# Adding the last block of the seven-product down step into x: from VectorE to a ScalarE copy and accumulating DMAs

## The chip, the core and the metric

The kernel runs on one core of a Trainium2 chip. The metric is the time of one launch in microseconds of the device. The core has TensorE (PE: matrix products into PSUM; its weight loads, PEld, run beside them), VectorE (DVE), ScalarE (ACT), GpSimd (POOL) and SyncE (SP). They run side by side, each its own list of instructions in order, and wait for one another by semaphores. Sixteen DMA engines move data; here SP issues the loads of the weights, and POOL issues the DMAs that add what they carry to what lies at their destination (accumulating DMAs).

## The reference, cut to what matters

The reference is one inference step of an encoder with two layers, for 512 new frames of one stream and 16 frames of each of eight running streams: 640 columns in all. Each layer is a half-step feed-forward block, a mixer (a short convolution and a banded attention with gates), and a second half-step feed-forward block:

```python
def _swiglu(h, w_gu, w_down):
    gu = h @ w_gu
    g, u = jnp.split(gu, 2, axis=-1)
    return (jax.nn.silu(g) * u) @ w_down
...
xp = xp + 0.5 * _swiglu(_rmsnorm(xp, norm_ffn1[l]), w_ffn1_gu[l], w_ffn1_down[l])
```

D_MODEL is 1024, D_FF is 2816, everything is float32. The change lies in the last product of this function, `@ w_down`, and in how its result, times a half, gets into x.

## The kernel before, in words

**Layout.** x lies in SBUF as eight tiles of 128 rows (of the 1024 features) by 640 columns (the frames). The columns are halved: `t1` is the first 320, `t2` the second. A float32 product is made of three faster ones: each operand is split into a high and a low part (`hi`, `lo`), and high x high, high x low and low x high are summed in PSUM.

**Weights.** One long stream of weights, laid out ahead, is loaded by SP (`load`, L236) into tiles `raw` of 512 KB, of which three exist. ACT copies the high part (`whi`, L296), DVE subtracts it from the tile to get the low part (`wlo`, L301); three tiles of each exist. When its `wlo` is done, a `raw` tile is free for the next load. SP's loads are in the order of the stream, and each waits for its buffer.

**Seven products for eight.** In most of the feed-forward blocks' steps a 2 x 2 block product is made with seven block products instead of eight (a Strassen-like scheme). Its blocks are named X11, X21, XN6, XT5, XT7, X22, XT4, and they are run in this order, each as 12 matmuls; each needs its own combination of weights and of activations. The combinations of weights are summed by DVE (`add`, L240; in the profile `s<-raw`, `s<-s,raw`, `raw<-raw,raw`, `raw<-s,raw`). A block's result goes into several outputs, so PSUM banks are read in the middle of their accumulation, and the next block on the same bank waits until that is done.

**Gate/up.** `gate_up` runs the seven blocks for one group of 128 features of the hidden layer: X11, XN6, XT7 and XT4 accumulate on one after the other in the bank `pa`, X21 in `pb`, XT5 and X22 in `pc`. ACT copies `pa` after X11 into c1 (L819). After XT7 DVE adds `pa` and the copy c5 into g (`add(g[:, t2], pa, c5)`, in the profile `ga<-paa,c_a` or `gb<-pab,c_b`), and XT4, the last block, goes on in `pa`. Between XT7 and XT4 there is one block, X22.

**Down.** `down_rows` does the same for four tiles of x at a time: its banks are A (`a`, two halves of 320 columns; `daa` and `dab` in the profile, for the two layers), B (`b`) and `c`. The results go into x in two ways. `take` is DVE: x = scale * bank + x, two instructions of 128 x 320 (L980). `stage` is ACT: a copy of the bank, with the factor, into a tile of SBUF with the tag `cap` (L967 for both halves of A in one instruction, L970 for the two c banks); then `send` issues two accumulating DMAs of 160 KB on POOL (L975), which add the two halves of the copy to two tiles of x. Before the change, of seven reads of the banks three are staged (c1 after X11, u2 after XN6, c5 after XT5) and four are takes (b after X21, a after XT7, c after X22, a after XT4). Three sends, that is six DMAs, belong to a call.

**Order.** The hidden features come in chunks, of four groups in the seven-product part. In a chunk the gate/up steps of this chunk and the down products of the chunk before are run in turn: gate/up, gate/up, down for x tiles 0 to 3 ("first call"), gate/up, down for x tiles 4 to 7 ("second call"), gate/up. There are 26 calls of `down_rows`, 13 first and 13 second, in four feed-forward blocks (6, 6, 8 and 6). In this part the order of PE's instructions is fixed by hand (`order({PE})`, a manual schedule of PE alone); where DVE's and ACT's instructions stand is decided by the Tile framework's scheduler, which places them by its own estimate of when each can run. `prep`, `flush`, `ahead` and `slab` are the functions that issue the weights' loads and splits a few blocks ahead.

Of the kernel before, what the change touches and what calls it, by code (L numbers as in the profile page):

```python
# [165 lines left out]
def two(ps):  # L166
    return ps[:, :, :HT]
# [7 lines left out]
def trunk(ctx: ExitStack, tc: tile.TileContext, xin, wst, small, pbias, samplebias, kcache, vcache,  # L175
# [24 lines left out]
    def acc(name):  # L200
        return banks["acc"].tile([P, 2, 512], F32, tag="acc", name=name)

    def att(name):
        return banks["att"].tile([P, 512], F32, tag="att", name=name)
# [78 lines left out]
    def prep(i):  # L283

        if i < len(ready) or i >= len(slabs):
            return
        assert i == len(ready)
        parts = source(i)
        hi = wp.tile([P, CH], F32R, tag="whi", name=f"whi{i}", bufs=3)
        lo = wp.tile([P, CH], F32R, tag="wlo", name=f"wlo{i}", bufs=3)  # L290
        ready.append((hi, lo))
        o = 0
        for src, c in parts:
            d = slice(o, o + c.stop - c.start)
            o = d.stop
            ACT.copy(hi[:, d], src[:, c])  # L296
            pending.append((lo[:, d], src[:, c], hi[:, d]))

    def flush():
        for lo, src, hi in pending:  # L300
            DVE.tensor_tensor(out=lo, in0=src, in1=hi.bitcast(F32), op=ALU.subtract)  # L301
        pending.clear()
# [3 lines left out]
    def slab(hold=False):  # L306

        flush()
        i = used[0]
        used[0] += 1  # L310
        while len(ready) < min(i + 2, len(slabs)):
            prep(len(ready))
            flush()
        prep(i + 2)
        if not hold:
            flush()
        return ready[i], slabs[i]

    def ahead():

        source(len(ready))

    def begin():

        prep(used[0] + 2)

    def quiet():

        used[0] += 1
        return ready[used[0] - 1]  # L330
# [599 lines left out]
    def step(later, place):  # L930

        for p in later:
            while p.done < 5 and p.spots[p.done] == place:
                next(p.work)
                p.done += 1

    def down_rows(fp, n, ms, pairs, tails, later):


        A, B = (acc(f"d{i}{n}") for i in "ab")  # L940
        a, b = ([z[:, u, :HT] for u in range(2)] for z in (A, B))
        c = [att(f"dc{n}_{u}")[:, :HT] for u in range(2)]
        t1, t2 = slice(0, HT), slice(HT, T)
        second = ms[0] > 0

        def mul(ps, s, half, kind, start):
            for u in range(2):
                for i, pair in enumerate(pairs):
                    kp = half * NP + 2 * u + i
                    wh, wl = (z[:, kp * P : (kp + 1) * P] for z in s)  # L950
                    xh, xl = pair.X[kind]
                    for j, (w, y) in enumerate(((wh, xh), (wh, xl), (wl, xh))):
                        PE.matmul(ps[u], w, y, start=start and i == 0 and j == 0,  # L953
                                  stop=i == 1 and j == 2, skip_group_check=True)

        def place(name):
            step(later, f"r{int(second)}{name}")

        def tail():
            for t in tails:  # L960
                t(False)
            tails.clear()

        def stage(name, ps, scale=0.5):
            z = fp.tile([P, 2, HT], F32, tag="cap", name=f"{name}{n}", bufs=5)
            if ps is A:
                ACT.activation(z, two(A), AF.Copy, scale=scale)  # L967
            else:
                for u in range(2):
                    ACT.activation(z[:, u], ps[u], AF.Copy, scale=scale)  # L970
            return z

        def send(z, r, cols):
            for u in range(2):
                POOL.dma_start(x[ms[2 * u + r]][:, cols], z[:, u], accum_op=ALU.add)  # L975

        def take(ps, r, cols, scale=0.5):
            for u in range(2):
                xs = x[ms[2 * u + r]][:, cols]
                DVE.scalar_tensor_tensor(out=xs, in0=ps[u], scalar=scale, in1=xs, op0=ALU.mult, op1=ALU.add)  # L980

        s0 = quiet()
        mul(a, s0, 0, X11, True)
        c1 = stage("c1_", A)
        prep(used[0] + 1)
        begin()
        if not second:
            tail()
        flush()
        place("d1")  # L990
        mul(b, s0, 1, X21, True)
        take(b, 0, t1)
        send(c1, 0, t1)
        s1 = slab(True)[0]
        flush()
        mul(a, s1, 0, XN6, False)
        u2 = stage("u2_", A)
        mul(c, s1, 1, XT5, True)
        c5 = stage("c5_", c, -0.5)
        s2 = slab(True)[0]  # L1000
        if second:
            tail()
        mul(a, s2, 0, XT7, False)
        take(a, 1, t2, -0.5)
        send(c5, 1, t2)
        flush()
        ahead()
        mul(c, s2, 1, X22, False)
        take(c, 0, t2)
        send(u2, 0, t2)  # L1010
        s3 = slab(True)[0]
        ahead()
        mul(a, s3, 0, XT4, False)
        take(a, 1, t1, -0.5)
        flush()

    def ffn(name, fp, ex, goff, after, end=False):
# [19 lines left out]
        for what, a in ffn_order(name):  # L1037
# [19 lines left out]
            if what == "rows":  # L1057
                ms, js = a
                down_rows(fp, f"{name}_{js[0]}_{ms[0]}", ms, [pairs[j] for j in js[::2]], tails, later)
                continue  # L1060
# [825 lines left out]
```

## Time and profile before

| | |
|---|---|
| median of 3 runs | 2536.31 us (2536.09 to 2536.59) |
| profiled execution | 2537.11 us, span 2535.3 us |
| TensorE's granted clock | 0.999 |
| busy: PE / DVE / ACT / POOL | 2512.6 / 2116.1 / 1271.9 / 198.1 us |
| DMA queue of POOL's software DMAs (q0) | 35.36 MB, 7.8% of 16 engines over the span |
| DMA queue of SP's loads (q1) | 223.90 MB, 27.3% |

The span is the time from the first to the last instruction of the profiled execution; what the whole execution took is 1.8 us more. A row of the groups reads: line, engine, operation, output <- inputs, count, duration in ns as min/median/max, first and last start in us, shape. A row of the waits reads: who waited, at which output and line, for whom; then the sum in us, how often, and the longest. A row of the timeline reads: start in us, duration in us, engine, line, operation, count; at its end, in brackets, how long the engine was idle before it and what ended that. A row of the DMA view with "KB" gives the line's transfers, their size, and the time from issue to landing. In the code after the change every line below L937 has a number higher by one.

### The profile page before, as it was taken

The page shows a single profiled execution, that of the slowest core. Times are in us where ns is not written, and L with a number is a line of the kernel's source. Part 1 is how long each engine was busy: PE and PEld are TensorE (multiplying, and loading weights), DVE is VectorE, ACT ScalarE, POOL GpSimd, SP SyncE. Part 2 cuts the span into 40 slices and gives each one's busy share as a digit, 9 for nine tenths or more (in the row PEclk, how much of TensorE's full clock was granted, in tenths as well). Part 3 has the DMA queues.
Part 4 walks back from the last instruction along what each step waited for, and adds up shares of the span by engine and source line. Part 5 has one row for each costly group of instructions (what it writes and reads, how often), then busy time and mean ns, then how long its engine had stood idle before and what let it go on. Part 6 is the DMA issues. An engine that isn't in the chain of part 4 may idle for free. (4 is left out here: it accounts for less than half of the span.)

```text
span 2535.3 us, 43090 instructions
## 1 busy us (share of the span) xinstructions
PE 2512.6 (99%) x17264; PEld 2451.2 (97%) x17264; DVE 2116.1 (83%) x3389; ACT 1271.9 (50%) x2010; POOL 198.1 (8%) x309
## 2 busy tenths in 40 slices
PE   8999999999999999999999999999999999999998
PEld 8999999888999999999999999998889999999998
DVE  7789998778777998998789999987786778999975
ACT  5345555664444545544455555556644445455543
POOL 0001111111000001110000111101110000011100
PEclk9999999999999999999999999999999999999999
DMA  3234343235222134443222444333442222244432
GB/s 135 67 100 115 108 121 112 106 112 171 76 76 92 64 112 113 107 110 99 84 84 92 120 118 115 105 105 118 134 137 84 76 85 78 97 115 115 116 99 75
DMA packets 96536, 262.65 MB, mean 104 GB/s; under 512 B 10736, under 2 KB 41584, under 8 KB 96336
## 3 DMA queue, kind: packets, MB, share of 16 engines
q1 hardware_dynamic: 70272, 223.90, 27.3%
q0 software_dynamic: 25344, 35.36, 7.8%
q8 instruction: 135, 2.21, 0.4%
q10 hardware_dynamic: 720, 0.65, 0.1%
q14 instruction: 65, 0.53, 0.1%
HBM read 225.85 MB, written 7.94 MB: 92 GB/s over the span
## 5 line engine op out<-in xcount | busy, mean ns | idle before, releaser
L296 ACT CAST whi<-raw 128x1024 fp32r<-128x1024 f32 (+1 forms) x566 | 506.1, 898 | 387.8 <-PE pcb L386 50.0
L301 DVE TENSOR_TENSOR wlo<-raw,whi 128x1024 fp32r<-128x1024 f32 (+1 forms) x566 | 581.7, 1031 | 120.8 <-ACT whi L296 115.2
L296 ACT CAST whi<-s 128x1024 fp32r<-128x1024 f32 (+1 forms) x146 | 138.0, 945 | 266.7 <-DVE s L240 113.8
L386 PE MATMUL pab<-xhib,whi 128*128 128x320 f32 x704 | 218.3, 310 | 1.3 <-DVE gb L240 1.0
L386 PE MATMUL pab<-xhib,wlo 128*128 128x320 f32 x704 | 217.2, 309 | 0.0
L386 PE MATMUL pab<-xlob,whi 128*128 128x320 f32 x704 | 217.2, 309 | 0.0
L386 PE MATMUL paa<-xhia,whi 128*128 128x320 f32 x640 | 198.0, 309 | 0.8 <-ACT c_a L766 0.6
L386 PE MATMUL paa<-xloa,whi 128*128 128x320 f32 x640 | 197.4, 308 | 0.0
L386 PE MATMUL paa<-xhia,wlo 128*128 128x320 f32 x640 | 197.4, 308 | 0.0
L301 DVE TENSOR_TENSOR wlo<-s,whi 128x1024 fp32r<-128x1024 f32 (+1 forms) x146 | 158.7, 1087 | 13.1 <-ACT whi L296 13.1
L386 PEld LDWEIGHTS pab<-xhib,whi 128*128 128x128 f32 x704 | 132.1, 188 | 2.5 <-DVE gb L240 1.2
L386 PEld LDWEIGHTS pab<-xlob,whi 128*128 128x128 f32 x704 | 132.1, 188 | 0.2
L386 PEld LDWEIGHTS pab<-xhib,wlo 128*128 128x128 f32 x704 | 132.1, 188 | 0.0
L240 DVE TENSOR_TENSOR s<-raw 128x512 f32<-128x512 f32 x110 | 75.7, 688 | 63.9 <-DMA raw<-in_wst 63.5
L386 PEld LDWEIGHTS paa<-xhia,whi 128*128 128x128 f32 x640 | 120.0, 187 | 1.6 <-ACT c_a L766 0.8
L975 POOL DMA_DIRECT2D x<-c_b x48 | 41.9, 956 | 1002.8 <-ACT whi L296 921.7
L386 PEld LDWEIGHTS paa<-xloa,whi 128*128 128x128 f32 x640 | 120.0, 188 | 0.1
L386 PEld LDWEIGHTS paa<-xhia,wlo 128*128 128x128 f32 x640 | 120.0, 187 | 0.0
L975 POOL DMA_DIRECT2D x<-c_a x56 | 49.1, 957 | 814.8 <-ACT whi L296 740.3
L386 PE MATMUL pcb<-xhib,whi 128*128 128x320 f32 x352 | 108.6, 309 | 0.0
L386 PE MATMUL pcb<-xlob,whi 128*128 128x320 f32 x352 | 108.6, 309 | 0.0
L386 PE MATMUL pcb<-xhib,wlo 128*128 128x320 f32 x352 | 108.6, 309 | 0.0
(686 smaller groups left out, 7894.7 us busy)
## 6 DMA issues: line engine op xcount, KB each, us to landing
raw<-in_wst SPq DMA_DIRECT2D x384, 512.0 KB, 3.5
x<-c_a POOLq DMA_DIRECT2D x56, 160.0 KB, 3.4
kc<-in_kcache SPq DMA_DIRECT2D x32, 256.0 KB, 4.0
vc<-in_vcache SPq DMA_DIRECT2D x16, 512.0 KB, 4.9
x<-c_b POOLq DMA_DIRECT2D x48, 160.0 KB, 3.4
x<-u_a POOLq DMA_DIRECT2D x28, 160.0 KB, 4.3
bias<-in_pbias POOLq DMA_DIRECT2D x16, 256.0 KB, 3.7
x<-u_b POOLq DMA_DIRECT2D x24, 160.0 KB, 4.4
```

The lines of the kernel that those rows point to most:

```text
L240: DVE.tensor_tensor(out=out, in0=a, in1=b, op=ALU.add)
L296: ACT.copy(hi[:, d], src[:, c])
L301: DVE.tensor_tensor(out=lo, in0=src, in1=hi.bitcast(F32), op=ALU.subtract)
L386: PE.matmul(ps, a, b, start=start and kp == 0 and j == 0, stop=stop and kp == NP - 1 and j == 2, skip_group_check=True)
L975: POOL.dma_start(x[ms[2 * u + r]][:, cols], z[:, u], accum_op=ALU.add)
```

## The change

The last read of bank A in `down_rows`, behind the block XT4, was a take by DVE: two instructions of 128 x 320 which add -0.5 times the bank to the first halves of two tiles of x. Now ACT copies the bank, times -0.5, into a new tile `c4_` with the tag `cap` in one instruction of 128 x 640, and POOL issues two accumulating DMAs of 160 KB. It is the same sum; x's tiles get it by another engine. Per call that is two DVE instructions fewer, one ACT instruction more and two POOL DMAs more.

```diff
@@ -937,6 +937,7 @@
     def down_rows(fp, n, ms, pairs, tails, later):
 
 
+
         A, B = (acc(f"d{i}{n}") for i in "ab")
@@ -1011,7 +1012,7 @@
         s3 = slab(True)[0]
         ahead()
         mul(a, s3, 0, XT4, False)
-        take(a, 1, t1, -0.5)
+        send(stage("c4_", A, -0.5), 1, t1)
         flush()
```

## The prediction

> **What bounds the kernel now.** I read the busy times first, then what PE waits for, then the timeline of the stretch around the changed step.
>
> ```profile
> span 2535.3 us, 43090 instructions
> PE 2512.6 (99%) x17264; PEld 2451.2 (97%) x17264; DVE 2116.1 (83%) x3389; ACT 1271.9 (50%) x2010; POOL 198.1 (8%) x309
> ```
>
> PE is busy for 2512.6 of 2535.3 us, and the change leaves its instructions and their order alone. So it can move the time only by what PE waits for. The rows of the waits that belong to the down products and the gate/up step behind them (times: sum in us, count, longest):
>
> ```profile
> PE daa L953 <- DVE x L980: 1.4, 7, 0.2
> PE dab L953 <- DVE x L980: 1.2, 6, 0.2
> PEld daa L953 <- DVE x L980: 3.2, 7, 0.5
> PEld dab L953 <- DVE x L980: 2.7, 6, 0.5
> PE pab L386 <- DVE gb L240: 1.0, 1, 1.0
> DVE s L240 <- DMA raw<-in_wst: 63.5, 37, 3.1
> ```
>
> PE stands at two kinds of place. The 13 stops of the first two rows are seen again at its weight loader, whose records overlap PE's, with 5.9 us, so that one costs about 0.46 us. The last row is DVE's own wait: 37 times it stands for a weight tile, 63.5 us in all. That is no loss yet, but PE waits for what stands behind it.
>
> The removed instructions, and the kind that takes their place on ACT:
>
> ```profile
> L980 DVE SCALAR_TENSOR_TENSOR x<-daa,x x56: 479/482/493, 221.2 to 1649.3; 128x320 f32<-128x320 f32 x56
> L980 DVE SCALAR_TENSOR_TENSOR x<-dab,x x48: 477/481/492, 977.8 to 2404.5; 128x320 f32<-128x320 f32 x48
> L967 ACT ACTIVATE c_b<-dab x12: 683/687/710, 970.7 to 2393.2; 128x640 f32<-128x640 f32 x12
> ```
>
> Half of the 104 go: two in each of 26 calls. Now one gate/up step behind such a call (the second call of its chunk). It starts at 323.53; its XT7 block starts at 330.57 and its XT4 block at 334.09, 3.52 us later:
>
> ```profile
> 323.73 0.89 DVE L980 SCALAR_TENSOR_TENSOR x<-daa,x 128x320 f32<-128x320 f32 x2
> ...
> 326.80 1.22 DVE L301 TENSOR_TENSOR wlo<-raw,whi 128x1024 fp32r<-128x1024 f32 x1
> 328.05 1.33 SPq L236 DMA_DIRECT2D raw<-in_wst  x2
> 330.57 0.31 PE L386 MATMUL paa<-xhia,whi 128*128 128x320 f32 x1
> 331.41 0.69 DVE L240 TENSOR_TENSOR s<-raw 128x512 f32<-128x512 f32 x1 [2.39 <-DMA raw<-in_wst]
> ...
> 333.15 0.48 DVE L240 TENSOR_TENSOR ga<-paa,c_a 128x320 f32<-128x320 f32 x1
> 333.55 0.68 DVE L240 TENSOR_TENSOR s<-s,raw 128x512 f32<-128x512 f32 x1
> 334.09 0.31 PE L386 MATMUL paa<-xhia,whi 128*128 128x320 f32 x1
> ```
>
> The reader is to see a chain. The end of `wlo<-raw` (328.02) frees a buffer, so SP issues the load (328.05); `s<-raw` waits for it until 331.41; behind it in DVE's queue stand a `wlo` and `ga<-paa`, and XT4 overwrites the bank that `ga<-paa` reads. That read ends at 333.63, so only 0.46 us are left.
>
> **The change part by part.** In the compiled order of the changed kernel PE and SP have the same instructions in the same order; DVE has 52 fewer, ACT 26 more, POOL 52 more.
>
> (1) The two takes. The pair holds DVE for up to 0.89 us from 323.73 on. DVE was behind here, so the two `wlo` and the buffer's release come up to that much earlier. Bounds: 0 (the next `wlo` waits for ACT instead) to 0.89. I take 0.7, since DVE had no idle time recorded between these rows.
>
> (2) The copy. 26 x 0.69 us on an ACT that is half idle. It waits for the same last product as the takes did. Behind it on ACT stand the `whi` of later weights and gate/up's c1 copy:
>
> ```profile
> 2404.07 1.05 ACT L296 CAST whi<-raw 128x1024 fp32r<-128x1024 f32 x1 [1.26 <-PE dab L953]
> 2405.84 0.43 ACT L819 COPY c_b<-pab 128x320 f32<-128x320 f32 x1 [0.72 <-PE pab L386]
> ```
>
> ACT was idle for 1.26 and 0.72 us there, so 0.69 us is taken up before c1. I take 0; were that cover gone, c1 could cost PE up to 0.69 x 26 = 18 us at XN6, which overwrites what c1 reads.
>
> (3) The two sends. POOL has only the sends to issue here:
>
> ```profile
> 2402.16 1.76 POOL L975 DMA_DIRECT2D x<-c_b  x2 [4.15 <-DVE x L980]
> 2403.30 2.40 POOL L975 DMA_DIRECT2D x<-u_b  x2
> ```
>
> The c4 pair stands behind the pair `x<-u_b`, and I put its issue at about 2.4 us more, which nobody waits for: the tile of x is next read much later, and ACT's tiles come around some 14 us apart (estimate from five buffers and about five copies to a call). What counts is the 16 DMA engines, where the pair meets the load of the chain above. Windows of the DMA view (20 quiet us; 10 us around four sends, two of u and two of c; two loads beside sends, packets of the queue or issue to landing in us):
>
> ```profile
> q1 hardware_dynamic: 431, 1.57, 25.8%
> raw<-in_wst SPq DMA_DIRECT2D x4, 512.0 KB, 3.4
> ```
> ```profile
> q0 software_dynamic: 583, 0.66, 44.4%
> ```
> ```profile
> raw<-in_wst SPq DMA_DIRECT2D x1, 512.0 KB, 4.2
> ```
> ```profile
> raw<-in_wst SPq DMA_DIRECT2D x1, 512.0 KB, 5.0
> x<-c_b POOLq DMA_DIRECT2D x2, 160.0 KB, 6.0
> ```
>
> A send is 128 packets; 583 took 44.4% of 10 us, so a pair (256) takes 4.44 x 256 / 583 = 1.95 us of all engines. A load alone lands in 3.4 us; beside sends in 4.2 (the gate/up from 2378.78, behind the tail of u2's pair) and 5.0 (two sends beside it). So a load that meets a whole pair is between 0 (if loads go first) and 1.95 us longer; I take 1.5, near the 5.0 row, because the c4 pair follows u2's directly and covers the load's whole time.
>
> [...]
>
> (4) DVE's order. Tile places DVE's instructions anew, and in the changed order the second sum `s<-s,raw` stands ahead of `wlo` and `g<-pa` in all 24 steps behind a call that have such a sum; before, in 6. One of those six shows the longer chain:
>
> ```profile
> 2385.82 0.31 PE L386 MATMUL pab<-xhib,whi 128*128 128x320 f32 x1
> 2386.04 0.69 DVE L240 TENSOR_TENSOR s<-raw 128x512 f32<-128x512 f32 x1 [2.30 <-DMA raw<-in_wst]
> 2386.77 0.69 DVE L240 TENSOR_TENSOR s<-s,raw 128x512 f32<-128x512 f32 x1
> 2387.38 1.22 DVE L301 TENSOR_TENSOR wlo<-raw,whi 128x1024 fp32r<-128x1024 f32 x1
> 2388.51 0.48 DVE L240 TENSOR_TENSOR gb<-pab,c_b 128x320 f32<-128x320 f32 x1
> ```
>
> From the start of `s<-raw` to the end of `gb<-pab` it is 2.95 us. PE therefore waits as soon as `s<-raw` starts later than 3.52 - 2.95 = 0.57 us behind XT7.
>
> (5) The 0.46 us stops ahead of the down products' own XT4 stay. They come from `take(a, 1, t2)`, which is not touched, and in the second calls the order ahead of it is the same:
>
> ```profile
> 2399.94 1.23 DVE L301 TENSOR_TENSOR wlo<-raw,whi 128x1024 fp32r<-128x1024 f32 x1 [0.46 <-ACT whi L296]
> 2401.09 0.88 DVE L980 SCALAR_TENSOR_TENSOR x<-dab,x 128x320 f32<-128x320 f32 x2
> 2402.02 0.41 PE L953 MATMUL dab<-t4hib,whi 128*128 128x320 f32 x1 [0.20 <-DVE x L980]
> ```
>
> In five first calls a sum moves ahead of this take and uses up the room; 0 to 0.5 us each, I take 0.
>
> The sum. Second calls: in 9 of the 11 with a sum `s<-raw` starts like the first, 331.41 - 330.57 = 0.84 us behind XT7, and up to 0.93. There the load met no send. The queue of the sends was as good as empty from 327.5 to 329.5:
>
> ```profile
> q0 software_dynamic: 6, 0.01, 2.0%
> ```
>
> So the load is longer by the whole 1.5 and starts 0.7 earlier: net +0.8, or +0.3 if a third of the pair is past by then. I take +0.6: the wait is 0.87 + 0.6 - 0.57 = 0.9 us, 9 x 0.9 = 8.1. The other two start earlier:
>
> ```profile
> 2410.58 0.69 DVE L240 TENSOR_TENSOR s<-raw 128x512 f32<-128x512 f32 x1 [1.73 <-DMA raw<-in_wst]
> ```
>
> XT7 there is at 2410.92; from -0.3 the load's 1.5 with little gain brings about +0.9, some 0.3 each, 0.6. First calls: 13 starts, the first and the last 0.17 and 0.22 behind XT7 (231.07 and 2385.82), all between -0.75 and 1.04, the middle one 0.48.
>
> ```profile
> 231.24 0.69 DVE L240 TENSOR_TENSOR s<-raw 128x512 f32<-128x512 f32 x1 [2.25 <-DMA raw<-in_wst]
> ```
>
> The load met u2's tail already (4.2), so only 5.0 - 4.2 = 0.8 is new and 0.7 is won: net +0.1 to +0.2. Only the four latest (0.57 to 1.04, mean 0.77) pass 0.57 clearly, by 0.35: 1.4, less what is only reached. Sum 8.1 + 0.6 + 1.4 = 10.1 us, and I take 9.5, since the sends may come in part behind the load. The profiled execution took 2537.11 us (span 2535.3 and 1.8 around it), 0.8 above the median of the runs; 2537.1 + 9.5 = 2546.6 answers to 2545.8 as a median. One in 500 (5.1 us) is about what a measurement can tell from no change.
>
> **The rivals.** (A) The load is hardly held, and the earlier release pays for it: a shift of -0.4 to 0. Then the moved sum alone costs 9 x (0.87 - 0.2 - 0.57) = 0.9 to 2.7 us and the first calls next to nothing: +2, 2538.3, no change. For it speaks that SP's load is issued up to 0.9 us earlier, at a time when u2's pair may be the only one in the engines; against it the 5.0 row. (B) The other side. The stops of (5) vanish because DVE, 0.9 us less laden, reaches `take(a, 1, t2)` in time: 13 x 0.46 = 6 us less, 2530.3. It decides if that take ends before PE's X22 block does. Against it: the `wlo` ahead of it waits 0.46 us for ACT, not for DVE's load of work. (C) The load waits for one send only, +1.0 instead of +1.5: shift +0.2 in the second calls, 9 x 0.5 = 4.5, first calls 1, 2541.8. [...] (D) The copy of (2) holds c1 or `whi` in every call: up to 18 us on top, 2555 or more. Against it stands ACT's idle time in front of both.
>
> **How the numbers follow.** Forecast 0.50 (2542.5 to 2551), (A) 0.17, (B) 0.06, (C) 0.20, (D) 0.07. Slower by over 0.2% (above 2541.4): the forecast, (D) and most of (C), 0.73. Within 0.2%: (A) and the rest of (C), 0.21. Faster 0.06. The range leaves out (B), the half of (A) that is below 2538, and the upper half of (D): 2538 to 2553.
>
> **What would show it.** In the changed profile: `g<-pa` of L240 as a releaser of PE's L386 some 10 to 20 times with about 0.5 to 1 us, in steps behind second calls first; `s<-raw` 0.3 to 0.8 us later behind XT7 there; the loads issued 0.6 to 0.8 us earlier but landing in 4.5 to 5 us; POOL near 250 us busy, DVE near 2091; the L953 stops still at 13. Wrong would be the forecast if those loads land in 3.5 us, or if XT4 of the down products no longer waits.

## The result, and the profile after

The changed kernel takes 2563.21 us (median; 2561.28 to 2563.46) against 2536.29 us: a ratio of 1.0102, 95% interval 1.009 to 1.0115. That is slower, as forecast, but by 27 us (26 between the profiled executions) and not by 9.5; it lies outside the range that was given (up to 2553). The profiled execution has a span of 2561.4 us, 26.1 more than before.

The page of the changed kernel, busy times:

```profile
span 2561.4 us, 43228 instructions
PE 2518.6 (98%) x17264; PEld 2451.5 (96%) x17264; DVE 2097.8 (82%) x3337; ACT 1290.7 (50%) x2036; POOL 244.7 (10%) x361
```

DVE is 18 us lighter, ACT 19 and POOL 47 us heavier, and PE has the same instructions. So again PE's waits must tell where 26 us are. Its weight loader shows them whole (us in total, times, longest); before, the only row like the first two was one stop of 1.2 us:

```profile
PEld paa L386 <- DVE ga L240: 14.4, 12, 2.0
PEld pab L386 <- DVE gb L240: 13.5, 12, 1.9
...
PEld daa L954 <- DVE x L981: 3.2, 7, 0.5
PEld dab L954 <- DVE x L981: 2.7, 6, 0.5
```

The reader is to see that 27.9 us stand at one kind of place, gate/up's XT4 waiting for `g<-pa`: 26.7 more than before, which covers the loss between the profiled executions (26.1). The stops of the down products' own XT4 (L953, now L954) are what they were, 13 times, 5.9 us.

What `g<-pa` stands behind is DVE's wait for the weights, which was 63.5 us before:

```profile
DVE s L240 <- DMA raw<-in_wst: 90.2, 34, 4.5
```

The step that the prediction showed (gate/up behind the second call; it started at 323.53, now at 326.16), timeline of the changed kernel:

```profile
328.42 1.22 DVE L301 TENSOR_TENSOR wlo<-raw,whi 128x1024 fp32r<-128x1024 f32 x1
329.67 1.82 SPq L236 DMA_DIRECT2D raw<-in_wst  x2
333.20 0.31 PE L386 MATMUL paa<-xhia,whi 128*128 128x320 f32 x1
335.58 0.69 DVE L240 TENSOR_TENSOR s<-raw 128x512 f32<-128x512 f32 x1 [4.46 <-DMA raw<-in_wst]
336.31 0.69 DVE L240 TENSOR_TENSOR s<-s,raw 128x512 f32<-128x512 f32 x1
336.92 1.22 DVE L301 TENSOR_TENSOR wlo<-raw,whi 128x1024 fp32r<-128x1024 f32 x1
338.05 0.48 DVE L240 TENSOR_TENSOR ga<-paa,c_a 128x320 f32<-128x320 f32 x1
338.59 0.41 PE L386 MATMUL paa<-xhia,whi 128*128 128x320 f32 x1 [1.71 <-DVE ga L240]
```

Counted from the start of the step, the load is issued at 3.51 us (before 4.52): the takes that are gone did bring it forward by 1.0 us. But `s<-raw` starts 2.38 us behind XT7 (333.20) and not 0.84. The sum that now stands ahead of `wlo` and `ga<-paa` is there, too, and PE waits 1.87 us: XT4 comes 5.39 us behind XT7 instead of 3.52. DVE, with less to do, stands idle for 4.46 us in front of a transfer.

What the load met is in the DMA view. The three stretches from the load's issue on, in the changed kernel (queue: packets, MB, share of 16 engines; 329.6 to 331, 331 to 333, 333 to 335.6):

```profile
q0 software_dynamic: 203, 0.23, 112.2%
...
q0 software_dynamic: 131, 0.15, 58.9%
q1 hardware_dynamic: 49, 0.20, 39.3%
...
q1 hardware_dynamic: 234, 0.84, 83.5%
q0 software_dynamic: 47, 0.04, 9.6%
```

Up to 331 not one packet of the load is moved, and all engines are on sends; its first one starts 1.62 us after the issue. Not all of that is the sends' doing. The kernel before had 6 packets of sends in the two us around its issue (328.05), and there, too, the load had no packet moved for 1.05 us (328 to 329, then 329 to 330):

```profile
q0 software_dynamic: 1, 0.00, 0.1%
```
```profile
q1 hardware_dynamic: 56, 0.23, 69.1%
```

From 331 to 333 the two queues share the engines, 58.9% of them with sends and 39.3% with the load, and the load gets 49 packets; only when the sends run out (47 packets from 333 on) does it get on, with 234.

### The profile page after: what moved, and what is told of

Read it like the earlier page. It is cut to its first block, busy times and chain, and to the rows that moved or that the text cites. A ratio compares the mean times of both kernels' runs of the same rounds, so it can differ in the third digit from the quotient of the medians.

```text
span 2561.4 us, 43228 instructions
## 1 busy us (share of the span) xinstructions
PE 2518.6 (98%) x17264; PEld 2451.5 (96%) x17264; DVE 2097.8 (82%) x3337; ACT 1290.7 (50%) x2036; POOL 244.7 (10%) x361
## 3 DMA queue, kind: packets, MB, share of 16 engines
q0 software_dynamic: 32832, 43.88, 10.0%
q8 instruction: 135, 2.21, 0.3%
## 4 chain that ended last, share of the span: by engine, by line
PE 82%; DVE 9%; DMA 3%; ACT 3%; issue 2%; SPq 0%; DVEq 0%; ACTq 0%
PE pab L386 10%; PE paa L386 9%; PE pcb L386 5%; PE pdb L363 5%; PE pca L386 4%; PE py L363 4%; PE po L363 4%; PE pda L363 4%; PE qa L386 4%; PE daa L954 4%; DMA raw<-in_wst 3%; PE dab L954 3%; DVE wlo L301 3%; PE pbb L386 2%; PE pba L386 2%; PE pv L1393 2%
## 5 line engine op out<-in xcount | busy, mean ns | idle before, releaser
L976 POOL DMA_DIRECT2D x<-c_b x72 | 68.7, 1147 | 994.2 <-ACT whi L296 711.9
L976 POOL DMA_DIRECT2D x<-c_a x84 | 80.1, 1142 | 807.2 <-ACT whi L296 461.0
```

## The experiments

For every run the table below gives how late `s<-raw` starts behind XT7 in the steps behind first and second calls (a mean over the 13 and 11 that have such a sum, from the timelines), since this is what the theories differ on. "W" is the theory that the collision of the load with the pair's sends costs the time; "O" that the moved sum does; "A" that ScalarE's copy does.

| kernel | time, us | ratio to before, 95% interval | s behind XT7, first / second, us |
|---|---|---|---|
| before | 2536.29 | | 0.29 / 0.67 |
| changed | 2563.21 | 1.0102 (1.009 to 1.0115) | 0.95 / 2.06 |
| no sends | 2536.96 | 0.9996 (0.9986 to 1.0006) | -0.27 / -0.16 |
| takes and one more pair | 2564.13 | 1.0101 (1.0086 to 1.0116) | 1.79 / 1.97 |
| copy, added by VectorE | 2537.44 | 1.0001 (0.9992 to 1.0011) | 0.30 / 0.44 |
| second calls only | 2556.1 | 1.0074 (1.0059 to 1.0089) | 0.01 / 2.07 |
| late sends | 2537.32 | 1.0002 (0.9992 to 1.0011) | -0.37 / -0.20 |
| one send of two | 2543.15 | 1.0024 (1.0014 to 1.0034) | 0.66 / 0.64 |
| plain copies | 2549.25 | 1.005 (1.0035 to 1.0066) | 0.94 / 0.84 |
| split read of bank A | 2530.91 | 0.9977 (0.9968 to 0.9986) | 0.26 / 2.21 |
| the same again | 2531.72 | 0.9979 (0.997 to 0.9988) | 0.26 / 2.19 |
| split read and late sends | 2530.95 | 0.9977 (0.9968 to 0.9986) | -0.18 / 0.22 |

The kernel before took 2536.86 to 2537.13 us beside the experiments.

**The sends taken out.**

```diff
-        send(stage("c4_", A, -0.5), 1, t1)
+        stage("c4_", A, -0.5)
```

> The changed kernel without the two accumulating DMAs of c4 (the copy is made and dropped, so the last block's share of x is left out); DVE's order is that of the changed kernel, with the sum ahead in 24 steps. Theory W (the load of weights behind a call lands only when the sends issued ahead of it are through, and the earlier release buys nothing while they run): with the pair gone the load meets no more sends than before and is issued up to 1 us earlier, s<-raw starts some 0.5 to 1 us sooner behind XT7 than before, the stops at XT4 vanish: 2534 to 2538 us. Rival O (the moved sum alone makes PE wait): over 2541, stops at XT4 stay by the dozen. Rival A (ScalarE's copy holds up what stands behind it): near 2563.

Measured 2536.96 us: no difference to before, though DVE's order is that of the changed kernel, with the sum ahead in all 24 steps. Its row for the load's wait, and the step behind the same call (it starts at 323.33, XT7 at 330.37):

```profile
DVE s L240 <- DMA raw<-in_wst: 54.3, 41, 2.7
```
```profile
326.84 1.80 SPq L236 DMA_DIRECT2D raw<-in_wst  x2
330.21 0.69 DVE L240 TENSOR_TENSOR s<-raw 128x512 f32<-128x512 f32 x1 [1.92 <-DMA raw<-in_wst]
```

The load is issued 3.51 us into the step as in the changed kernel and `s<-raw` starts 3.4 us after that. With the sends it took 5.9 us to the same point (329.67 to 335.58). The load's first packet is moved 0.96 us after the issue here, in place of 1.62. So O and A fall as causes of the 26 us (for O with one limit: `s<-raw` starts ahead of XT7 here, and what the moved sum would cost with `s<-raw` as late as before was not run), and the prices can be read off: the two takes away are worth 0.56 us (first calls, 0.29 to -0.27) and 0.83 us (second, 0.67 to -0.16) of earlier landing; the pair of sends costs 1.22 us (-0.27 to 0.95) and 2.22 us (-0.16 to 2.06).

**The sends added to the kernel before.**

```diff
         take(a, 1, t1, -0.5)
+        send(u2, 1, t1)
```

> The kernel before, with its takes, and one more pair of accumulating DMAs of the same size at the place of c4's (u2's copy is sent a second time, so x gets a wrong share). DVE's order and work are those of before. Theory W: the load meets the same backlog of sends, so s<-raw starts as late as in the changed kernel (2 us or more behind XT7 in second calls); only the sum does not stand ahead of g, which leaves 0.7 us more room at each of some 18 stops: 2547 to 2555 us. Rival O: 2536 (no change). Rival A: 2536.

Measured 2564.13 us, as slow as the changed kernel, with DVE's work and order unchanged from before. The collision alone makes the loss: in the profiled execution, with 2560.77 us the fastest of its four, gate/up's XT4 stops at the weight loader sum to 23.2 us. It is more than W gave (2547 to 2555), for a reason that the last column shows. In second calls `s<-raw` is as late as in the changed kernel (1.97 and 2.06), although the load is released about 1 us later: there the earlier release buys nothing against the sends. In first calls it is 1.79, against 0.95: there the release is worth 0.84. What the sum's old place saves in second calls is lost again in first ones: by the distance of XT4 from XT7 (beyond 3.52 us) the stops sum to 10.1 us behind first and 9.8 behind second calls, in the changed kernel to 7.8 and 17.1 (each from one profiled execution). Of the 7.3 us between the two sums for second calls, 1.0 is the later `s<-raw` (0.09 x 11); the rest, 6.3 us, falls to the nine second calls in which the sum has moved, 0.70 each. That is an estimate of the price of the order once the load is late; without the pair's sends, with `s<-raw` ahead of XT7, it costs nothing.

**The copy without DMAs.**

```diff
-        send(stage("c4_", A, -0.5), 1, t1)
+        c4 = stage("c4_", A, -0.5)
+        for u in range(2):
+            xs = x[ms[2 * u + 1]][:, t1]
+            DVE.tensor_tensor(out=xs, in0=c4[:, u], in1=xs, op=ALU.add)
```

> ScalarE copies the bank as in the changed kernel, but VectorE adds the copy to x from SBUF, with no DMAs; DVE's order in the steps behind a call is that of before. Theory W: 2535 to 2539 us, the copy costs nothing. Rival A: near 2563, or at least 2550. Rival O: 2536.

Measured 2537.44 us, no difference. ScalarE's 26 copies are hidden; A falls by itself.

**Second calls only.**

```diff
-        send(stage("c4_", A, -0.5), 1, t1)
+        if second:
+            send(stage("c4_", A, -0.5), 1, t1)
+        else:
+            take(a, 1, t1, -0.5)
```

> Only the 13 second calls of each chunk take the new path; first calls keep the takes. Theory W: the stops of the second calls stay (in the changed kernel they sum to about 17 of 25 us by XT7-to-XT4 spacing beyond 3.52), those of the first calls go: 2552 to 2555 us. Rival O (the order has moved in 15 of 24 steps): a share by count, 2549 to 2553. If calls all cost the same: 2549.5.

Measured 2556.1 us: 19 of the 27 us are made behind 13 of the 26 calls. The stops behind second calls are the same as in the changed kernel (17.2 us by the distance), those behind first calls are none. It is a little more than W gave (2552 to 2555). The stops at its weight loader are 18.7 us more than before (19.9 against 1.2), which is near the 19 us of the medians; the profiled execution itself was the longest of its four (2560.4 us, 23.3 over before), and the other 4.6 us of it are not explained:

```profile
PEld pab L386 <- DVE gb L240: 11.6, 8, 2.4
PEld paa L386 <- DVE ga L240: 8.3, 6, 2.4
```

**The same sends, later.** In the changed kernel the pair waits for gate/up's copy c5, by way of a two-column instruction that adds nothing:

```diff
-        send(stage("c4_", A, -0.5), 1, t1)
+        c4 = stage("c4_", A, -0.5)
+        def rest(c5):
+            DVE.scalar_tensor_tensor(out=c4[:, :, 0], in0=c5[:, 0:2], scalar=0.0,
+                                     in1=c4[:, :, 0], op0=ALU.mult, op1=ALU.add)
+            send(c4, 1, t1)
+        late.append(rest)
...
             ACT.copy(c5, pc)
             s2 = slab(True)[0]
+            for f in late:
+                f(c5)
+            late.clear()
```

> The changed kernel, but c4's two sends wait until the copy c5 of the gate/up step behind the call is made (a two-column VectorE instruction, which adds nothing to c4, holds them), so that they are issued when the load of weights has landed or nearly so. All DMAs and all sums are those of the changed kernel. Theory W (what costs is that the load meets the pair's backlog in the DMA engines): 2535 to 2540 us, s<-raw near or ahead of XT7 again as without the sends. Rival N (the number of accumulating DMAs costs by itself, wherever they lie): near 2563.

Measured 2537.32 us: the whole loss is gone with all the DMAs still there. Its queue of sends, and its one stop at gate/up's XT4:

```profile
q0 software_dynamic: 32832, 43.88, 9.9%
```
```profile
PE pab L386 <- DVE gb L240: 0.6, 1, 0.6
```

The same 43.88 MB as in the changed kernel. N falls: not the number of transfers costs, but where they lie.

**One send of two.**

```diff
-        send(stage("c4_", A, -0.5), 1, t1)
+        c4 = stage("c4_", A, -0.5)
+        POOL.dma_start(x[ms[1]][:, t1], c4[:, 0], accum_op=ALU.add)
+        xs = x[ms[3]][:, t1]
+        DVE.tensor_tensor(out=xs, in0=c4[:, 1], in1=xs, op=ALU.add)
```

> Of c4's two sends one is made; VectorE adds the other half of the copy from SBUF. Theory W: the load is some 1.2 us later in place of 2.5 (against a kernel without the pair) and released half as much earlier; the second calls then start s<-raw some 1.5 us behind XT7, 0.3 to 0.9 us too late: 2541 to 2550 us, less than half of the 26 us, since the room is used up first. If the price is by count: 2549.5.

Measured 2543.15 us: half the transfers cost 6 us, a quarter of the loss. In second calls `s<-raw` is then no later than before (0.64). But this is not the changed kernel with half the sends alone: DVE's order differs, too. The sum has moved ahead behind all 13 first calls, but behind two of the 11 second ones only (as before), so XT4 has more room there. By the distance the stops are 3.7 us behind first and 1.8 behind second calls. That the first part of a delay is taken by the room fits these numbers; how much of the step from 6 to 27 us is due to it, and how much to the order, is not told apart.

**Plain copies.**

```diff
-        send(stage("c4_", A, -0.5), 1, t1)
+        c4 = stage("c4_", A, -0.5)
+        for u in range(2):
+            POOL.dma_start(x[ms[2 * u + 1]][:, t1], c4[:, u])
```

> The changed kernel with c4's two DMAs as plain copies of the same size on the same queue, not accumulating (they overwrite their part of x, so that is left out of the sum). If accumulation is what makes a pair hold the engines for 2 us (each element read twice): the load is about 1 us less late and the time 2541 to 2550 us. If it is the queue, the packets' number and their size: 2560 to 2565 us, as changed.

Measured 2549.25 us, 12 us over before. The load is 1.00 us later in second calls than without sends (-0.16 to 0.84), in place of 2.22; in first calls it is 1.21, as much as with accumulation (1.22). So a copy of the same bytes without accumulation delays the load less than half as much behind second calls, and no less behind first ones. But the DMAs differ in more than the adding, as the queue's row shows (27840 packets in the profile of this kernel):

```profile
q0 software_dynamic: 27840, 43.88, 8.8%
```

Against 25344 of the kernel before, 52 plain DMAs are 2496 packets, 48 each; the 52 accumulating ones of the changed kernel are 7488, 144 each. Whether it is the accumulation or the number and size of the packets that makes the difference is not told apart; that each element is read twice was a supposition, and no view shows it: the queue's row has 43.88 MB for both kinds.

**The split read.** This one starts from the kernel before and goes at the other stop of its profile, the 0.46 us ahead of the down products' XT4 in second calls:

```diff
-        take(a, 1, t2, -0.5)
+        if second:
+            c7 = stage("c7_", A, -0.5)
+            for v in range(2):
+                xs = x[ms[2 * v + 1]][:, t2]
+                DVE.tensor_tensor(out=xs, in0=c7[:, v], in1=xs, op=ALU.add)
+        else:
+            take(a, 1, t2, -0.5)
```

> The kernel before (all takes, no c4), but in second calls the read of bank A behind XT7 is split: ScalarE copies it to SBUF, and VectorE adds the copy to x later; so XT4 of the down products waits for a copy on a half-idle ScalarE and no longer for VectorE's two instructions. The stops of 0.46 us at 13 places should go: 2530.5 us (2529 to 2534). Rival: VectorE's adds only move behind and delay the release of the load's buffer, so that stops appear at gate/up's XT4 in their place: 2535 to 2540.

Measured 2530.91 us, 0.9977 (0.9968 to 0.9986): faster than both kernels, by what the 13 stops were worth (5.9 us). No wait of the down products for VectorE is left among PE's waits. In this kernel's order `g<-pa` stands ahead of `s<-raw` behind nine of the second calls, so a late `s<-raw` (2.21 in the table) holds nothing. That order came with the edit, so the gain is that of the split together with it.

**Both.** The split read and the late sends in one kernel, and the split read again beside it.

> The late sends of c4 together with the split read of bank A behind XT7 in second calls. Theory W: taking the two instructions per call off VectorE is worth nothing, as nothing that PE waits for is left behind them; the split read alone gives its 6 us: 2530 to 2533 us, the same as the split read with the takes. Rival G (VectorE's relief has a worth of its own once the collision is gone): below 2529.

> The split read alone once more, beside the former on the same chip: 2530.9 us as measured (2529 to 2533), no stop of the down products' XT4 left.

Measured 2530.95 and 2531.72 us, their intervals of the ratio nearly the same. Freeing VectorE of two instructions per call is worth nothing measurable even when the sends do no harm; G falls.

## Why the prediction was wrong

- **What bounds, and where.** Right: PE waits at gate/up's XT4 for `g<-pa`, 24 times by the weight loader's rows and 20 by PE's own (10 to 20 were named), most of it behind second calls, because `s<-raw` waits for the load; the 26.7 us there cover the span's 26.1.
- **(1) The takes.** Right in size: 0.56 and 0.83 us of earlier landing where no sends follow (0.7 taken). In the step shown the issue came 1.0 us forward, a little past the bound of 0.89. What was wrong is what became of it, see (3).
- **(2) The copy.** Right: nothing.
- **(3) The sends, and the net with (1).** This is the step that failed: "longer by the whole 1.5 and starts 0.7 earlier", taken as +0.6 net behind second calls, and 0.8 less 0.7, +0.1 to +0.2, behind first ones. Measured are 1.39 (0.67 to 2.06) and 0.66 (0.29 to 0.95). Four kernels of the table, with and without the takes and the pair, tell the two terms apart:

| s behind XT7, first / second, us | no pair | with the pair | price of the pair |
|---|---|---|---|
| with the takes (later issue) | 0.29 / 0.67 | 1.79 / 1.97 | 1.50 / 1.30 |
| without them (earlier issue) | -0.27 / -0.16 | 0.95 / 2.06 | 1.22 / 2.22 |
| worth of the earlier issue | 0.56 / 0.83 | 0.84 / -0.09 | |

Behind second calls 1.5 was about right for a load issued as late as before (1.30), but nothing may be taken off it: a load that is issued earlier meets more of the same sends. Between the load's issue and its landing the sends held the engines for 1.9 us at the later issue and for 2.9 us at the earlier one (means over the 11 steps); in the step shown, first with the takes and one more pair (331.48 to 336.54, 42.4% of 5.06 us, 2.1 us), then in the changed kernel (329.67 to 335.49, 50.1% of 5.82 us, 2.9 us):

```profile
q0 software_dynamic: 259, 0.29, 42.4%
```
```profile
q0 software_dynamic: 371, 0.41, 50.1%
```

Behind first calls the 0.7 does come off (0.84), but the pair's price was 1.50 and not 0.8. The 0.8 took the 4.2 us row for the time of a load that meets u2's tail. In the profile before, four loads behind first calls met about 0.8 us of sends; they landed in 3.2, 3.3, 4.1 and 4.2 us, and two that met less than 0.1 us of sends landed in 4.0 and 4.2. So that row was not the price of the tail. What else makes a load land later is not shown.

The bound was wrong, too. The 583 packets of its window are four sends of 144 packets (by the queue's counts above; the 128 that were taken leave out 16 of under 512 B: the pages count 832 more of these after the change, with 52 sends more) and a few more, so a pair is half of 4.44, 2.2 us of all engines and not 1.95. The 2.22 that was measured lies at that. In the step shown the load lands 2.5 us later than without the pair (5.9 against 3.4). Of this, 0.66 us is the later first packet (1.62 against 0.96), and the 178 packets of sends from 331 on are 1.4 us of work. The rest goes while both queues are in the engines: from 331 to 333 they were in use for 98% and moved 131 packets of sends and 49 of the load, by the rates of the windows in the prediction (4.44 us for 583, 5.16 us for 431) 1.0 + 0.6 = 1.6 us of work in 2 us (an estimate).

- **(4) The order.** Right: the room was 0.51 us in the step shown (2.38 - 1.87), 0.57 had been worked out; the moved sum costs nothing without the pair's sends, and about 0.70 us per second call once the load is late (an estimate, from 6.3 us over nine calls), near its own duration of 0.69.
- **(5)** Right: the 13 stops stayed, 5.9 us.
- **The sum.** Second calls: 2.06 - 0.57 = 1.5 us by 11 is 16.4 (by the distance 17.1); the prediction had 9 x 0.9 + 0.6 = 8.7. First calls: 7.8 in place of 1.4, since 0.66 us instead of 0.1 to 0.2 of net delay puts eleven of 13 past the room, not four. A net delay off by 0.8 and 0.5 us made 24.9 us of stops by the distance out of the 10.1 forecast, because the room was already used up.
- **The rivals.** (A), hidden, fell: the earlier release does not pay for the sends. (B), the other side, fell: the stops of (5) stayed; the split read shows what they were worth. (C), the load waits for one send only (+1.0, half of the pair's 1.95), fell: the time was 2563.21 us and not 2541.8, and the pair's price was 2.22 us behind second calls and 1.22 behind first ones. That a load waits for one send of the pair alone was a supposition; no run shows it. (D), the copy, gave a time near the measured one for a reason that the third experiment rules out.

Open is how the engines share between the two queues in detail, why the earlier issue keeps its worth behind first calls and not behind second ones, and how much of a send's price is the accumulation.

## What to carry to other kernels

An accumulating DMA that takes work off a busy engine is not free because its own queue is nearly empty on average (7.8% here): look at what else is in the DMA engines in the two or three microseconds after its issue, above all a load that something in order waits for. The same transfers cost 26 us or nothing, by whether they were issued ahead of the load or behind it. Price a load that meets a backlog by the work of all sends that are still to come at its issue, those of the instructions just ahead included (2.9 us here behind second calls, of which 2.2 were paid; that the 1.05 us without a packet, which the load had in the kernel before as well, hide the rest is a guess). Do not take an earlier issue off that price without looking at what it will meet; it was worth nothing behind second calls (-0.09 us) and 0.84 us behind first ones. And where the waiter has only half a microsecond of room (0.51 us in the step shown), multiply every further tenth by the number of places.

## What was not expected of the hardware

- In the step shown, a load of 512 KB that was issued while accumulating DMAs filled the engines (112.2% from 329.6 to 331) reached the instruction that waits 5.9 us after its issue; without the pair's sends in 3.4 us. Its first packet was moved 1.62 us after the issue, and even with the engines idle (the kernel before, 0.1% from 328 to 329) only after 1.05 us.
- With both kinds in the engines, they moved about a fifth less than at the rates of the prediction's windows (an estimate from the two us of one step: 1.6 us of work in 2 us).
- An accumulating DMA of 160 KB inside SBUF was made of 144 packets (7488 for the 52 of the changed kernel), a plain one of the same tiles of 48 (2496 for the 52 of the plain copies).
